# Gate and up of two feed-forward layers, from the fifth feature tile on, as pairs of output tiles by seven half-size products

## The chip, the cores and the metric

One core of a Trainium2 chip runs the whole program. The time is the device time of one execution, in microseconds. Profiles come from one further execution.

## What is computed

A decoder layer on 512 tokens of width 1024: a half-weighted SwiGLU feed-forward layer (FFN1), two parallel attention mixers, cross-attention to a memory of 256 rows, a second SwiGLU layer (FFN2), and a last norm. Only the two feed-forward layers change. D_FF is 2816.

```python
def swiglu(h, w_gate, w_up, w_down):
    return (jax.nn.silu(h @ w_gate) * (h @ w_up)) @ w_down
...
x = x + 0.5 * swiglu(rms_norm(x, norm_ffn1[l]), w1_gate[l], w1_up[l], w1_down[l])
...
x = x + 0.5 * swiglu(rms_norm(x, norm_ffn2[l]), w2_gate[l], w2_up[l], w2_down[l])
return rms_norm(x, norm_final)
```

## The kernel before

The activations lie transposed, features on the 128 partitions and the 512 tokens along the columns. A weight tile `w1_gate[f]` is 128 x 1024: for each of 8 k blocks of the input, the 128 output features of tile f. There are 22 feature tiles, FT.

Every product keeps float32 accuracy in three passes. An operand is split into a high half (a cast to float32r on ScalarE, L77) and a low half (a subtraction on VectorE, L78), and high x high, high x low, low x high are added up in one PSUM bank (`dense_steps`, L94 to L104). `wload` (L84) loads a weight tile on SP's queue into one of three raw buffers `wr` and splits it in pieces of 512 columns into `wh`, `wl` (two buffers each); it is given a priority 40 instructions ahead.

In `ffn` (L204) a feature tile is 24 matmuls of 512 columns for gate and 24 for up, with the weights stationary and `xh`, `xl` moving. `xh`, `xl` are x times the norm's gain, split (L201, L202); the norm's row factor `rb` is applied afterwards: t1 = gate x rb (L217), Silu (L219), times rb (L220), times up (L223), split into `ah`, `al`. The down part then makes 8 output tiles m, each from 66 matmuls: 22 f x 3 passes. In FFN2 the last output tile is made in two halves of 256 tokens (L234 to L241) and the final norm follows each half (`finish`, L946).

The homes of the tiles matter below. Group B (`big`, L70) has 30 buffers of 2 KB a partition: x, and of `ah`, `al` those with f < 11. The other `ah`, `al` are in the FFN's own pool (L205, L210). `xh`, `xl` have 16 tiles of their own (L137, L138).

A scheduler sets each engine's order at build time: by readiness, and among what is ready by place in the program, less the priority. An engine then takes its instructions in that order. In the trace, for example, the first matmuls of the mixing stage stand ahead of the sums of the norm before it.

`tables` (L276) is FFN1's hook. After tile 5 it makes bias tables with four small matmuls (L297), copies them from PSUM (L298), writes them to DRAM (L299, L300) and spreads them there to 128 rows a head, `fa_r` and `fb_r` (L301, L302), all on POOL's queue. After FFN1 x goes to DRAM (`x_d`, L307), and the mixing stage projects `xh`, `xl` with w_in.

Of the kernel before, what the change touches and what calls it, by code (L numbers as in the profile page):

```python
# [9 lines left out]
F32 = mybir.dt.float32  # L10
F32R = mybir.dt.float32r
AF = mybir.ActivationFunctionType
ALU = mybir.AluOpType
# [19 lines left out]
VC = 408  # L33
DOWN = (8, 8, 6)
OFF = (0, 128, 384, 768)
NB = 30
AHEAD = 40
LB = 3
PB = 3
# [9 lines left out]

SLOT_A = "STSffTSfPSTSfPTffPfP"  # L50
SLOT_B = "fSSfTTSfffPP"
GRP = ((0,), (1,), (2, 3))


@with_exitstack
def hybrid_layer(ctx: ExitStack, tc: tile.TileContext, a: dict):
# [13 lines left out]
    def big(dt, name):  # L70
        return g.tile([P, S], dt, tag="B", name=name, bufs=NB)

# [33 lines left out]
    def dense(*args):  # L106
        for _ in dense_steps(*args):
            pass
# [29 lines left out]
    xl = [g.tile([P, S], F32R, name=f"xl{k}") for k in range(KT)]  # L138

    class Norm:  # L140
        def __init__(self, width, tag, nsq=1, tsq=None, tacc=None):
# [62 lines left out]
    def ffn(pool, tag, rb, nrm, gi, first=None, hook=None, done=None):  # L204
        def act(n):  # L205
            return pool.tile([P, S], F32R, tag="act", name=n, bufs=2 * FT - (NB - KT))

        ah, al = [], []
        for f in range(FT):
            mk = act if 2 * f >= NB - KT else (lambda n: big(F32R, n))  # L210
            ah.append(mk("ah"))
            al.append(mk("al"))
            pg, pu = bank("d"), bank("d")
            fg, fu = first if first and f == 0 else (None, None)
            dense(pg, [(a[f"w{tag}_gate"][f], KT)], xh, xl, fg)
            t1 = pool.tile([P, S], F32, tag="t1", name="t1", bufs=2)
            V.tensor_mul(t1, pg, rb())  # L217
            s1 = pool.tile([P, S], F32, tag="s1", name="s1", bufs=2)
            A.activation(s1, t1, AF.Silu)  # L219
            V.tensor_mul(s1, s1, rb())  # L220
            dense(pu, [(a[f"w{tag}_up"][f], KT)], xh, xl, fu)
            ac = pool.tile([P, S], F32, tag="ac", name="ac", bufs=2)
            V.tensor_mul(ac, pu, s1)  # L223
            split(ah[f], al[f], ac)
            if hook:
                hook(f)
        for m in range(KT):
            pd = bank("d")
            src = a[f"w{tag}_down"][m]
            ch, o = [], 0  # L230
            for n in DOWN:
                ch.append((src[:, o * P:(o + n) * P], n))
                o += n
            if done and m == KT - 1:  # L234
                for c0 in (0, S // 2):
                    c = slice(c0, c0 + S // 2)
                    dense(pd[:, :S // 2], ch, [t[:, c] for t in ah], [t[:, c] for t in al])
# [19 lines left out]
    with tc.tile_pool(name="f1", bufs=1, reuse_waits="tile") as pool:  # L257
        first = [wpair(), wpair()]

        def part(i, c0, c1):  # L260
            h, l = first[i]
            split(h[:, c0:c1], l[:, c0:c1], raw0[i][:, c0:c1])

        part(0, 0, 256)
        for k in range(KT):
            scale_split(xh[k], xl[k], x[k], gain(0, k))
            if k < 3:
                part(*((1, 0, 256), (0, 256, 1024), (1, 256, 1024))[k])
        n1 = Norm(S, "x", 3)
        for k in range(KT):  # L270
            n1.feed(pool, x[k])
        n1.finish()

        tb = {}

        def tables(f):  # L276
            if f == 0:
                tb["rel"] = pool.tile([33, 16], F32, name="rel")
                tb["oh32"] = pool.tile([P, FA + FB], F32, name="oh32")
                nc.gpsimd.dma_start(tb["rel"], a["rel"])  # L280
                nc.gpsimd.dma_start(tb["oh32"], a["oh"])
            if f != 5:
                return
            rel, oh32 = tb["rel"], tb["oh32"]
            rr = pool.tile([P, 16], F32R, name="rr")
            oh = pool.tile([P, FA + FB], F32R, name="oh")
# [644 lines left out]
        n4.finish()  # L931


    n5 = Norm(S, "x", 3)
    with tc.tile_pool(name="f2", bufs=1, reuse_waits="tile") as pool:
        gx = []
        halves = [[], []]

        def turn(half, i, ks):
            if len(halves[half]) <= i:  # L940
                halves[half].append(bank(("ssot", "ddds")[half][i]))
            for k in ks:
                c = (k - 4 * half) * P
                T.transpose(halves[half][i][:, c:c + P], gx[k][:, i * P:(i + 1) * P], ident)  # L944

        def finish(c0):  # L946
            c = slice(c0, c0 + S // 2)
            tiles = range(c0 // P, c0 // P + 2)
            m = KT - 1
            sq = pool.tile([P, S // 2], F32, tag="sqx", name="sq", bufs=3)  # L950
            A.activation(sq, x[m][:, c], AF.Square)
            V.tensor_scalar(gx[m][:, c], x[m][:, c], gain(4, m), None, op0=ALU.mult)
            for i in tiles:
                turn(1, i, range(4, m))
            st = n5.sums2(sq, c0)
            for i in tiles:
                turn(1, i, (m,))
            r = n5.rstd(st, 2)
            for i in tiles:
                o = pool.tile([P, D], F32, tag="out", name="out", bufs=2)  # L960
                rr = r[:, i % 2:i % 2 + 1]
                A.activation(o[:, :512], halves[0][i], AF.Copy, scale=rr)
                V.tensor_scalar(o[:, 512:], halves[1][i], rr, None, op0=ALU.mult)  # L963
                if c0:
                    nc.scalar.dma_start(a["out"][i * P:(i + 1) * P, :512], o[:, :512])
                    nc.sync.dma_start(a["out"][i * P:(i + 1) * P, 512:], o[:, 512:])
                else:
                    (nc.sync if i % 2 else nc.scalar).dma_start(a["out"][i * P:(i + 1) * P, :], o)

        def done(m, c0=0):  # L970
            if c0 == 0:
                gx.append(pool.tile([P, S], F32, tag=("t1", "t1", "s1", "s1", "ac", "ac", "t1", "t1")[m],
                                    name="gx", bufs=2))
# [9 lines left out]
        ffn(pool, "2", lambda: n4.rb, n5, None, done=done)  # L983


OUT = (S, D)
# [94 lines left out]
```

## Time and profile before

| | us |
|---|---|
| median of 3 runs | 1292.76 (1291.57 to 1292.77) |
| the profiled execution, its own time | 1293.45 |
| its span | 1291.4 |
| TensorE busy | 1272.5 |
| VectorE busy | 717.4 |
| ScalarE busy | 569.0 |
| 139 MB moved by DMA, mean | 108 GB/s |

FFN1 lies at 5 to 377 us of the span, the mixing stage from there to 751, cross-attention to about 917, FFN2 after it. Matmul rows overlap, so TensorE's pace is read from the distance between two starts, not from a row's length. A row of the timeline may merge several instructions (x2).

### The profile page before, as it was taken

Reading aid. Unit: us, or ns where it says so; the run is one execution under the profiler, and the core shown is the slowest. Engines: PE = TensorE matmul, PEld = TensorE weight load, DVE = VectorE, ACT = ScalarE, POOL = GpSimd, SP = SyncE. Lnnn points to the kernel's source line nnn. Section 1 sums busy time; section 2 is a strip of 40 time slices with the busy share of each in tenths; the row PEclk is TensorE's granted clock in tenths of the full one; section 3 lists DMA queues with packets and bytes.
Section 4 is the critical chain, followed back from the end, with each engine's and each line's share of the span. In section 5 each row is a group of like instructions: output and inputs, shape, how many; then the busy total and the mean of one; then the engine's idle time right before and its main releaser. Section 6 shows DMA issues by size and latency. Waiting matters only on the chain. (4 is left out here: it accounts for less than half of the span.)

```text
span 1291.4 us, 16177 instructions
## 1 busy us (share of the span) xinstructions
PE 1272.5 (99%) x6092; PEld 1057.6 (82%) x6092; DVE 717.4 (56%) x1510; ACT 569.0 (44%) x1178; POOL 29.9 (2%) x56
## 2 busy tenths in 40 slices
PE   7999999999999999999999999999999999999997
PEld 5888888888887888888888898887888888888887
DVE  5554444433348787887878666465544444443334
ACT  6333333322234677776784454444433333322223
POOL 0000000000020000000001000000000000000000
PEclk9999999999999999999999999999999999999999
DMA  5346333233343531222225345212233333332233
GB/s 205 98 131 236 97 98 97 93 118 111 106 142 97 177 97 65 88 71 70 62 92 164 111 137 173 82 50 82 82 98 98 98 98 98 98 94 90 90 97 116
DMA packets 41199, 139.11 MB, mean 108 GB/s; under 512 B 6248, under 2 KB 6512, under 8 KB 41120
## 3 DMA queue, kind: packets, MB, share of 16 engines
q1 hardware_dynamic: 34704, 120.04, 29.6%
q0 software_dynamic: 5840, 16.95, 3.8%
q8 instruction: 48, 0.79, 0.2%
q10 hardware_dynamic: 576, 1.07, 0.2%
q14 instruction: 31, 0.25, 0.1%
HBM read 133.80 MB, written 10.07 MB: 111 GB/s over the span
## 5 line engine op out<-in xcount | busy, mean ns | idle before, releaser
L77 ACT ACTIVATE wh<-wr 128x512 fp32r<-128x512 f32 (+1 forms) x456 | 259.8, 614 | 598.0 <-issue 389.3
L102 PE MATMUL ps_d<-xh,wh 128*128 128x512 f32 x1000 | 393.1, 394 | 8.0 <-ACT xh L201 8.0
L102 PE MATMUL ps_d<-xh,wl 128*128 128x512 f32 x1000 | 393.0, 393 | 1.7 <-DVE wl L78 1.7
L102 PE MATMUL ps_d<-xl,wh 128*128 128x512 f32 x1000 | 391.9, 392 | 0.0
L78 DVE TENSOR_TENSOR wl<-wr,wh 128x512 fp32r<-128x512 f32 (+1 forms) x456 | 291.5, 674 | 150.9 <-ACT wh L77 148.7
L102 PEld LDWEIGHTS ps_d<-xh,wh 128*128 128x128 f32 x1000 | 188.6, 189 | 46.3 <-ACT xh L201 9.4
L102 PEld LDWEIGHTS ps_d<-xh,wl 128*128 128x128 f32 x1000 | 188.6, 189 | 39.3 <-DVE wl L78 2.1
L102 PEld LDWEIGHTS ps_d<-xl,wh 128*128 128x128 f32 x1000 | 188.4, 188 | 38.1 <-DVE xl L202 1.0
L102 PE MATMUL ps_d<-ah,wl 128*128 128x512 f32 (+1 forms) x374 | 142.3, 380 | 0.0
L102 PE MATMUL ps_d<-al,wh 128*128 128x512 f32 (+1 forms) x374 | 142.2, 380 | 0.0
L102 PE MATMUL ps_d<-ah,wh 128*128 128x512 f32 (+1 forms) x374 | 142.0, 380 | 0.0
L223 DVE TENSOR_TENSOR ac<-ps_d,s 128x512 f32<-128x512 f32 x44 | 30.4, 691 | 123.1 <-PE ps_d L102 123.1
L217 DVE TENSOR_TENSOR t<-ps_d,rb 128x512 f32<-128x512 f32 x44 | 30.4, 691 | 123.0 <-PE ps_d L102 120.7
L102 PEld LDWEIGHTS ps_d<-al,wh 128*128 128x128 f32 x374 | 70.3, 188 | 14.4
L102 PEld LDWEIGHTS ps_d<-ah,wh 128*128 128x128 f32 x374 | 70.3, 188 | 14.3
L102 PEld LDWEIGHTS ps_d<-ah,wl 128*128 128x128 f32 x374 | 70.3, 188 | 13.9
L481 ACT ACTIVATE pth<-ps_t 128x512 fp32r<-128x512 f32 (+1 forms) x64 | 32.6, 524 | 18.3 <-PE ps_t L586 15.4
L482 DVE TENSOR_TENSOR ptl<-ps_t,pth 128x512 fp32r<-128x512 f32 (+1 forms) x64 | 37.8, 602 | 3.5 <-ACT pth L481 2.8
L542 DVE CUSTOM_DVE_ANT_0 L<-ps_s,strA 128x512 f32<-128x512 f32 (+1 forms) x64 | 31.0, 485 | 13.5 <-PE ps_s L499 13.3
L544 ACT ACTIVATE L<-L,ms 128x512 f32<-128x512 f32 (+1 forms) x64 | 35.5, 556 | 6.1 <-DVE ms L542 5.9
L498 PE MATMUL ps_s<-kkh,qs 128*128 128x256 f32 (+7 forms) x104 | 31.6, 320 | 0.3 <-DVE ms L542 0.3
L220 DVE TENSOR_TENSOR s<-s,rb 128x512 f32<-128x512 f32 x44 | 30.1, 684 | 1.3 <-ACT s L219 1.3
(268 smaller groups left out, 1553.1 us busy)
## 6 DMA issues: line engine op xcount, KB each, us to landing
wr<-in_w_gate_dram SPq DMA_DIRECT2D x43, 512.0 KB, 3.5
wr<-in_w_up_dram SPq DMA_DIRECT2D x43, 512.0 KB, 3.5
wr<-in_w_down_dram SPq DMA_DIRECT2D x34, 512.0 KB, 3.5
wr<-in_w_in_dram SPq DMA_DIRECT2D x29, 512.0 KB, 3.5
wr<-in_w_down_dram SPq DMA_DIRECT2D x17, 384.0 KB, 3.0
fa_r<-fa_d POOLq DMA_DIRECT2D x1, 4160.0 KB, 34.2
wr<-in_cw_dram SPq DMA_DIRECT2D x8, 512.0 KB, 3.6
wr<-in_w_out_dram SPq DMA_DIRECT2D x8, 512.0 KB, 3.6
```

The lines of the kernel that those rows point to most:

```text
L77: A.activation(h, src, AF.Copy)
L78: V.tensor_sub(l, src, f32(h))
L102: yield T.matmul(out, w[:, c], m, start=i == 0, stop=i == total - 1)
L217: V.tensor_mul(t1, pg, rb())
L220: V.tensor_mul(s1, s1, rb())
L223: V.tensor_mul(ac, pu, s1)
L481: A.activation(h[:, :n], pt[:, :n], AF.Copy)
L482: V.tensor_sub(l[:, :n], pt[:, :n], f32(h[:, :n]))
L498: first = T.matmul(out, q[:, tk], kk[0][:, ks], start=True, stop=False)
L542: V.tensor_tensor_reduce(sl, sc, hd["strip"][:, (3 - i) * P:512], -1.0, BIG, ALU.add, ALU.min, ms[:, i:i + 1])
L544: A.activation(sl, sl, AF.Exp, bias=ms[:, i:i + 1], scale=-1.0, accum_out=ss[:, i:i + 1])
```

## The change

In both FFNs the feature tiles 0 to 3 are made as before. From tile 4 on two neighbouring feature tiles f, f+1 are taken together. The product of a 2 x 2 block matrix (two output tiles by two halves of the input features, 4 k blocks each) with a 2 x 2 block matrix (two halves of the input features by two halves of the tokens, 256 each) is made from seven products of blocks instead of eight. A product is 4 k x 3 passes = 12 matmuls of 256 columns. There are 18 such steps q in an FFN, gate and up in turn.

The blocks of the activations, their sums and the halves of both are made once, after tiles 0 and 1 (`prepare`); they contain gain and rb, so nothing is multiplied by rb later. Blocks b11, b21, b22 lie in group B, the sums t3, t4, n2, n1 in the pool's new tag E. The sums of weight blocks are made per step: two by a load (`s31`, from SP) onto which a second load is added by a DMA with an add, from POOL's queue, and two by additions on VectorE (`s2`, `s4`). The weights of a step are split in 3584 columns, not 2048. Partial products are used twice, so ScalarE copies them from bank to bank and the matmuls go on from there; two matmuls ahead of the loop prepare the two banks.

Group B has 46 buffers instead of 30 and also holds `xh`, `xl`, which are given up after tile 3 and made again at the end of FFN1, and `ah`, `al` with f < 15. The tables of FFN1 are made after tile 1 instead of tile 5, in three parts. The down part makes its tiles 0 and 1 side by side, chunk by chunk.

```diff
-NB = 30
+NB = 46
+NE = 23
+NSTD = 4
+NEARLY = 4
...
-    xh = [g.tile([P, S], F32R, name=f"xh{k}") for k in range(KT)]
+    xh = [big(F32R, f"xh{k}") for k in range(KT)]
...
+        def prepare(i):
+            ys = []
+            for k0 in (2 * i, 2 * i + 4):
+                y = pool.tile([P, 1024], F32, tag="S", name="y", bufs=3)
+                for j in range(2):
+                    V.scalar_tensor_tensor(y[:, j * S:(j + 1) * S], x[k0 + j], gain(gin, k0 + j), nrm_in.rb,
+                                           op0=ALU.mult, op1=ALU.mult)
+                ys.append(halves(y))
...
+            V.tensor_sub(v["n1"], ta, tb_)
+            V.tensor_sub(v["t3"], bb, tb_)
+            V.scalar_tensor_tensor(v["n2"], v["n1"], -1.0, bb, op0=ALU.mult, op1=ALU.subtract)
+            V.scalar_tensor_tensor(v["t4"], v["n2"], -1.0, ba, op0=ALU.mult, op1=ALU.subtract)
+            for n, src in (("b11", ta), ("b21", ba), ("b22", bb)):
+                h, l = big(F32R, n), big(F32R, n)
+                A.activation(halves(h), src, AF.Copy)
+                V.tensor_sub(halves(l), src, halves(f32(h)))
+            for n in ("t3", "t4", "n2", "n1"):
+                h, l = ext(n, F32R), ext(n, F32R)
+                split(h, l, sums[n])
...
+        def load(q):
...
+            nc.sync.dma_start(d["r1"], w[f])
+            d["s"] = pool.tile([P, 1024], F32, tag="S", name="s31", bufs=3)
...
+            nc.sync.dma_start(s31, bass.AP(o.tensor, o.offset, [[1024, P], [0, 2], [1, 512]]))
+            o = w[f]
+            nc.gpsimd.dma_start(s31, bass.AP(o.tensor, o.offset, [[1024, P], [P * 1024 + 512, 2], [1, 512]]),
+                                accum_op=ALU.add)
...
+        def product(out, w, c0, n, start=False):
+            i = 0
+            for k in range(4):
+                c = slice(c0 + k * P, c0 + (k + 1) * P)
+                bh, bl = (t[:, k % 2 * 256:k % 2 * 256 + 256] for t in blk[n][k // 2])
+                for ww, m in ((w[0], bh), (w[0], bl), (w[1], bh)):
+                    T.matmul(out, ww[:, c], m, start=start and i == 0, stop=i == 11, skip_group_check=True)
+                    i += 1
...
+        load(0)
+        load(1)
+        load2(0)
+        for _ in range(2):
+            t = bank("s")
+            T.matmul(t, xh[0][:, :P], xl[0], start=True, stop=True, skip_group_check=True)
+        s2(0)
+        h1(0)
+        h2(0)
+        early = list(range(NEARLY))
+        for q in range(NQ + 1):
...
+            if d:
+                x_, g_ = bank("d")[:, :256], bank("s")
+                product(x_, d["h1"], 0, "b11", True)
+                A.activation(g_[:, :256], x_, AF.Copy)
+                h3(q)
+                if q + 2 < NQ:
+                    load(q + 2)
+                if q + 1 < NQ:
+                    s2(q + 1)
+                p7 = bank("o")[:, :256]
+                product(p7, d["h2"], 0, "t3", True)
...
+                if q + 1 < NQ:
+                    h1(q + 1)
+            if e:
+                join_b(q - 1)
+                product(e["x"], e["h4"], 512, "t4")
+                join_a(q - 1)
+            if d:
+                s4(q)
+                product(x_, d["h2"], 512, "n2")
+                A.activation(g_[:, 256:], x_, AF.Copy)
+                if q + 1 < NQ:
+                    h2(q + 1)
+                product(g_[:, :256], d["h1"], 512, "b21")
+            if e:
+                product(e["g"][:, 256:], e["h4"], 0, "b22")
+                out_g(q - 1)
+            if d:
+                h4(q)
+                if q + 1 < NQ:
+                    load2(q + 1)
+                if early:
+                    act_split(early.pop(0))
+                product(g_[:, 256:], d["h3"], 0, "n1")
...
+        if not done:
+            for m in range(KT):
+                xh[m], xl[m] = big(F32R, f"xh{m}"), big(F32R, f"xl{m}")
+                scale_split(xh[m], xl[m], x[m], gain(gi, m))
...
-            if f != 5:
+            if f != 1:
```

`h1` to `h4` split the weights of a step (h1: the whole tile f, 1024 columns; h2: 2 x 512; h3: 512; h4: 1024), `join_a` and `join_b` add the copied product p7 in halves of 256 columns, `out_g` makes Silu or the product with it for tile f, and `load2` loads 256 KB of tile f+1 for h4. h2, h3, h4 have one buffer each, tag S has three.

## Rows read from the trace of the kernel before

**Rows 1.** The page: busy time of the engines (us, share of the span, instructions)

```profile
PE 1272.5 (99%) x6092; PEld 1057.6 (82%) x6092; DVE 717.4 (56%) x1510; ACT 569.0 (44%) x1178; POOL 29.9 (2%) x56
```

**Rows 2.** Timeline, TensorE in FFN1's gate and up: start, length, engine, line, operation

```profile
99.70 0.39 PE L102 MATMUL ps_d<-xh,wh 128*128 128x512 f32 x1
...
121.46 0.39 PE L102 MATMUL ps_d<-xh,wh 128*128 128x512 f32 x1
```

**Rows 3.** Stretches of FFN1: busy time of each engine, clock, DMA share, GB/s

```profile
88.00:125.00 37.00, 37.00 (x165) 30.65 (x164) 16.44 (x27) 10.65 (x20) 2.18 (x2) 1.00 0.75 258
125.00:200.00 75.00, 75.00 (x333) 62.10 (x332) 34.91 (x56) 23.34 (x42) 0.00 (x0) 1.00 0.30 95
```

**Rows 4.** Timeline, 256 columns in FFN2's last down tile; weight loads of the key projection

```profile
1264.96 0.28 PE L102 MATMUL ps_d<-ah,wh 128*128 128x256 f32 x1
...
1268.82 0.28 PE L102 MATMUL ps_d<-ah,wh 128*128 128x256 f32 x1
...
1272.65 0.28 PE L102 MATMUL ps_d<-ah,wl 128*128 128x256 f32 x1
...
L102 PEld LDWEIGHTS ps_d<-gh,wh x64: 187/188/192, 751.4 to 776.0; 128*128 128x128 f32 x64
```

**Rows 5.** Timeline, 512 columns in FFN2's down tile 6

```profile
1249.74 0.40 PE L102 MATMUL ps_d<-ah,wh 128*128 128x512 f32 x1
...
1257.45 0.40 PE L102 MATMUL ps_d<-ah,wh 128*128 128x512 f32 x1
...
1259.53 0.39 PE L102 MATMUL ps_d<-ah,wh 128*128 128x512 f32 x1
...
1264.51 0.39 PE L102 MATMUL ps_d<-al,wh 128*128 128x512 f32 x1
```

**Rows 6.** Groups by line and shape: one of three groups of 1000 with `xh`, `xl`

```profile
L102 PE MATMUL ps_d<-xh,wh 128*128 128x512 f32 x1000 | 393.1, 394 | 8.0 <-ACT xh L201 8.0
```

**Rows 7.** Groups by shape on VectorE and ScalarE (busy us, mean ns); two timeline rows

```profile
L78 DVE TENSOR_TENSOR wl<-wr,wh 128x512 fp32r<-128x512 f32 x431 | 281.4, 686 | 148.3 <-ACT wh L77 146.1 <-PE ps_o L494 1.6
L77 ACT ACTIVATE wh<-wr 128x512 fp32r<-128x512 f32 x431 | 250.7, 624 | 597.6 <-issue 389.3 <-PE ps_d L102 182.4 <-PE ps_d L855 9.8
L579 ACT ACTIVATE pth<-ps_t 128x256 fp32r<-128x256 f32 x8 | 3.0, 371 | 0.6 <-PE ps_t L577 0.6
...
14.34 3.40 DVE L202 SCALAR_TENSOR_TENSOR xl<-x,gains,xh 128x512 fp32r<-128x512 f32 x5
37.79 1.28 DVE L78 TENSOR_TENSOR wl<-wr,wh 128x512 fp32r<-128x512 f32 x2
```

**Rows 8.** Timeline, VectorE in FFN2: first use of rb, and output of tile 3

```profile
923.95 0.69 DVE L217 TENSOR_TENSOR t<-ps_d,rb 128x512 f32<-128x512 f32 x1 [0.47 <-ACT rb L193]
...
960.75 0.69 DVE L223 TENSOR_TENSOR ac<-ps_d,s 128x512 f32<-128x512 f32 x1 [2.95 <-PE ps_d L102]
```

**Rows 9.** Timeline, VectorE in FFN1: first use of rb, outputs of tiles 1 and 3

```profile
29.84 0.69 DVE L217 TENSOR_TENSOR t<-ps_d,rb 128x512 f32<-128x512 f32 x1 [1.88 <-ACT rb L193]
...
37.18 0.69 DVE L223 TENSOR_TENSOR ac<-ps_d,s 128x512 f32<-128x512 f32 x1 [1.15 <-PE ps_d L102]
...
58.94 0.69 DVE L223 TENSOR_TENSOR ac<-ps_d,s 128x512 f32<-128x512 f32 x1 [2.94 <-PE ps_d L102]
```

**Rows 10.** The tables: timeline of TensorE and POOL, then DMA issues (KB, us to landing)

```profile
80.50 0.63 PE L297 MATMUL ps_t<-oh,rr 128*8 128x512 f32 x2
...
88.84 1.09 POOL L301 DMA_DIRECT2D fa_r<-fa_d  x1 [3.04 <-DMA fa_d<-fa]
90.07 1.09 POOL L302 DMA_DIRECT2D fb_r<-fb_d  x1
...
fa_r<-fa_d POOLq DMA_DIRECT2D x1, 4160.0 KB, 34.2
fb_r<-fb_d POOLq DMA_DIRECT2D x1, 1536.0 KB, 33.8
wr<-in_w_gate_dram SPq DMA_DIRECT2D x43, 512.0 KB, 3.5
```

More of the change, by code (lines that the diff above doesn't have):

```diff
@@ L135, in hybrid_layer @@
     V.memset(ones, 1.0)
-    xh = [g.tile([P, S], F32R, name=f"xh{k}") for k in range(KT)]
-    xl = [g.tile([P, S], F32R, name=f"xl{k}") for k in range(KT)]
+    xh = [big(F32R, f"xh{k}") for k in range(KT)]
+    xl = [big(F32R, f"xl{k}") for k in range(KT)]
     class Norm:
@@ L202, in scale_split, with ffn, ext, act_split @@
         V.scalar_tensor_tensor(l, src, gcol, f32(h), op0=ALU.mult, op1=ALU.subtract)
[L204 to L212, printed above, removed]
+    def ffn(pool, tag, nrm_in, gin, nrm, gi, first=None, hook=None, done=None):
+        def ext(name, dt=F32):
+            return pool.tile([P, S], dt, tag="E", name=name, bufs=NE)
+        wsrc = {"g": a[f"w{tag}_gate"], "u": a[f"w{tag}_up"]}
+        act, ah, al = [None] * FT, [None] * FT, [None] * FT
+        def act_split(f):
+            ah[f], al[f] = (big(F32R, n) if f < 15 else ext(n, F32R) for n in ("ah", "al"))
+            split(ah[f], al[f], act[f])
+        blk = {n: [None, None] for n in ("b11", "b21", "b22", "n1", "t3", "n2", "t4")}
+        def halves(t):
+            return t.rearrange("p (j c) -> p j c", j=2)
+        def prepare(i):
[6 more added lines that the diff above has]
+                ys.append(halves(y))
+            yt, yb = ys
+            ta, tb_, ba, bb = yt[:, :, :256], yt[:, :, 256:], yb[:, :, :256], yb[:, :, 256:]
+            sums = {n: big(F32, n + "s") for n in ("n1", "t3", "n2", "t4")}
+            v = {n: halves(t) for n, t in sums.items()}
+            V.tensor_sub(v["n1"], ta, tb_)
[6 more added lines that the diff above has]
+                V.tensor_sub(halves(l), src, halves(f32(h)))
+                blk[n][i] = h, l
+            for n in ("t3", "t4", "n2", "n1"):
+                h, l = ext(n, F32R), ext(n, F32R)
+                split(h, l, sums[n])
+                blk[n][i] = h, l
+        for f in range(NSTD):
@@ L213, in ffn @@
             pg, pu = bank("d"), bank("d")
             fg, fu = first if first and f == 0 else (None, None)
[L215 to L218, printed above, removed]
+            dense(pg, [(wsrc["g"][f], KT)], xh, xl, fg)
+            t1 = ext("t1")
+            V.tensor_mul(t1, pg, nrm_in.rb)
+            s1 = ext("s1")
@@ L219, in ffn @@
             A.activation(s1, t1, AF.Silu)
[L220 to L224, printed above, removed]
+            V.tensor_mul(s1, s1, nrm_in.rb)
+            dense(pu, [(wsrc["u"][f], KT)], xh, xl, fu)
+            act[f] = big(F32, "act")
+            V.tensor_mul(act[f], pu, s1)
             if hook:
                 hook(f)
-        for m in range(KT):
-            pd = bank("d")
-            src = a[f"w{tag}_down"][m]
+            if f in (0, 1):
+                prepare(f)
@@ new lines, in load2, with hl, s2, s4 @@
+        def load2(q):
+            w, f = pairs[q]
+            q_[q]["r2"] = pool.tile([P, 1024], F32, tag="R2", name="r2", bufs=1)
+            nc.sync.dma_start(q_[q]["r2"][:, 512:], wsrc[w][f + 1][:, 512:])
+        def hl(tag_, n):
+            return tuple(pool.tile([P, n], F32R, tag=tag_ + z, name=tag_ + z, bufs=1) for z in "hl")
+        def s2(q):
+            d = q_[q]
+            d["s2"] = ext("s2")
+            V.tensor_add(d["s2"], d["s"][:, 512:], d["r1"][:, :512])
+        def s4(q):
+            d = q_[q]
+            V.tensor_add(d["r2"][:, :512], d["s2"], d["r1"][:, 512:])
@@ L230, in ffn, with chunks, finish_m @@
+        def chunks(m):
             ch, o = [], 0
             for n in DOWN:
-                ch.append((src[:, o * P:(o + n) * P], n))
+                ch.append((a[f"w{tag}_down"][m][:, o * P:(o + n) * P], n))
                 o += n
+            return ch
+        def finish_m(m, pd):
+            V.scalar_tensor_tensor(x[m], pd, 0.5, x[m], op0=ALU.mult, op1=ALU.add)
+            if done:
+                done(m)
+            else:
+                nrm.feed(pool, x[m])
+        two = [bank("d"), bank("d")]
@@ new lines, in ffn @@
+        o = 0
+        for c, n in enumerate(DOWN):
+            ws = [wload(*(lambda z: (z[0], z[1] * P))(chunks(m)[c])) for m in range(2)]
+            for f in range(o, o + n):
+                if ah[f] is None:
+                    act_split(f)
+            for m in range(2):
+                h, l = ws[m]
+                for kk in range(n):
+                    cc = slice(kk * P, (kk + 1) * P)
+                    f = o + kk
+                    for z, (w, v) in enumerate(((h, ah[f]), (h, al[f]), (l, ah[f]))):
+                        T.matmul(two[m], w[:, cc], v, start=f == 0 and z == 0, stop=f == FT - 1 and z == 2)
+            o += n
@@ L234, in ffn @@
+        for m in range(2):
+            finish_m(m, two[m])
+        for m in range(2, KT):
+            pd = bank("d")
             if done and m == KT - 1:
@@ L949, in finish @@
             m = KT - 1
-            sq = pool.tile([P, S // 2], F32, tag="sqx", name="sq", bufs=3)
+            sq = pool.tile([P, S], F32, tag="E", name="sq", bufs=NE)[:, :S // 2]
             A.activation(sq, x[m][:, c], AF.Square)
@@ L959, in finish @@
             for i in tiles:
-                o = pool.tile([P, D], F32, tag="out", name="out", bufs=2)
+                o = pool.tile([P, D], F32, tag="S", name="out", bufs=3)
                 rr = r[:, i % 2:i % 2 + 1]
@@ L971, in done @@
             if c0 == 0:
-                gx.append(pool.tile([P, S], F32, tag=("t1", "t1", "s1", "s1", "ac", "ac", "t1", "t1")[m],
-                                    name="gx", bufs=2))
+                gx.append(big(F32, "gx"))
             if m == KT - 1:
@@ L981, in done @@
                     turn(0, i, range(4))
-        ffn(pool, "2", lambda: n4.rb, n5, None, done=done)
+        ffn(pool, "2", n4, 3, n5, None, done=done)
 OUT = (S, D)
```

105 lines of the change are left out of this document (79 added, 26 removed).

## The prediction

> **What bounds the kernel now.** I read the page first: TensorE is busy for 1272.5 us, 99% of the span [rows 1], and its granted clock is 1.00 in the stretches that I read [rows 3]. A busy matmul row is no measure of pace, because the rows overlap (394 ns long, while a new one starts every 227 ns), so next I took start-to-start pitches from the timeline. In gate and up, 96 consecutive pitches take 121.46 - 99.70 = 21.76 us, 226.7 ns each, without a hole [rows 2]. That stretch is bound by TensorE alone: what shortens the matmul stream shortens the kernel, until something else comes late. VectorE works 34.9 of 75 us there, ScalarE 23.3, the DMA engines 30% [rows 3].
>
> The profiled execution took 1293.45 us, 0.7 above the median 1292.76; the sum is made against it and 0.7 is taken off at the end.
>
> **The matmul stream.** Per FFN, 18 of the 22 feature tiles become 9 pairs, each for gate and for up: 18 steps. A step had 2 x 24 = 48 matmuls of 512 columns, 48 x 226.7 ns = 10.88 us. It gets 7 products x 4 k x 3 passes = 84 of 256 columns. The kernel has such matmuls already. In FFN2's last down tile the first 33 start from 1264.96 to 1268.82, 117.0 ns apart; their moving halves `ah`, `al` (f < 11) lie in group B. The next 32 pitches, to 1272.65, are 119.7 ns; those halves lie in the FFN pool [rows 4]. After the change three moving blocks (b11, b21, b22) lie in B and four (t3, t4, n2, n1) in the pool's tag E, so I take 36 x 116.8 + 48 x 119.9 ns = 9.96 us a step. It saves 0.92 us, **36 steps: -33.1 us**, where the bare count of columns (1/8 of 36 x 10.88) would promise 49: the pitch at half width is more than half. A weight load row before a matmul of that width is 188 ns long [rows 4], yet these matmuls follow each other in 117, so loads overlap and don't set the pace.
>
> The Trainium skill (TensorE: Matmul & The Clock Gate, Back-to-back issue gap) gives N/2.4 + 2.5 ns, which is 109 and 216 ns here. By it the steps would save 36 x (48 x 215.8 - 84 x 109.2 ns) = 42.7 us. The trace differs at both widths, so the rows' pitches stand.
>
> **The moving operand's home.** `xh` and `xl` had tiles of their own and now come from group B. At 512 columns B is the slower home: in down tile 6 of FFN2 the 33 matmuls from B take 1257.45 - 1249.74 = 7.71 us, 233.6 ns each, those from the pool 4.98/22 = 226.4 [rows 5], as with `xh` in its own tiles [rows 2]. There are 3 x 1000 matmuls with `xh` or `xl` [rows 6]; the FFNs hold 2112, of which 384 stay (four tiles), and 888 are in w_in and w_xq. So 1272 x 6.7 ns = **+8.5 us**; nothing if it isn't the group that makes it. `ah`, `al` for f 11 to 14 move to B as well: 4 x 3 x 8 x 6.7 ns = 0.64 a FFN, **+1.3**. Two warm-up matmuls a FFN: **+0.9**.
>
> **Inside a step.** VectorE: a 512-column subtraction is 0.69 us, 0.60 behind another (two take 1.28) [rows 7]. A step has seven for the low halves, two sums, two joins of half the width (0.35, half of 0.69) and one output on average: 6.7 to 7.6 of 9.96 us. ScalarE: 7 x 0.62 + 3 x 0.37 + 0.62 = 6.1. Both fit. A copy of a partial product has at least two products (2.8 us) until the next accumulation. The tightest is h4: its buffer is free after product b22, it is read three products (4.3 us) later, and it needs a Silu (0.62), a cast of 1024 (two of 0.62 at most) and a subtraction (1.2), 3.1 us. It is covered, except in the last step, where only n1 (1.4 us) lies between: **+1.2 a FFN, +2.4** (0 to 4).
>
> The loads become 1.75 MB a step (512 KB whole, 512 KB base, 512 KB added to it from POOL's queue, 256 KB), 184 GB/s against 95 at 30% [rows 3]: 58% of the engines if an adding byte costs as a plain one, 75% at twice. No row shows an adding DMA; plain is the nearest (3.5 us for 512 KB [rows 10]). I take twice, which adds nothing to the sum, as plain wouldn't; four times is rival 3. SP's queue is used in order, but the loads are issued a step ahead.
>
> **The end of FFN1.** `xh`, `xl` take the buffers of `ah`, `al`, so their scaling comes after the last down tile. The next stage's matmuls need them one k block after another; half of the 16 buffers are free before that, the others as tile 7 reads them. I take 0, at worst 3.
>
> **The start of FFN2.** rb is there at 923.95, tile 3 ends at 960.75 [rows 8]: 36.8 us. VectorE owes 12 operations x 0.6 for the four tiles, five weight tiles x 1.2, the `prepare` work (2 x (6 x 0.68 + 9 x 0.60) = 19.0, the 0.68 being 3.40 us for five [rows 7]) and the first sums and halves (1.8): 34.0. It fits: **+0.5** (0 to 3).
>
> **The start of FFN1.** There rb comes when tile 1 is nearly done: 29.84, and tile 3 ends at 58.94 [rows 9], 29.1 us. VectorE owes 7.2 + four weight tiles 4.8 + 19.0 + table copies 2.0 + 1.8 = 34.8. `prepare(0)` stands ahead of tile 2's weight split, so TensorE waits there: **+5.5** (3 to 8). The steps then begin at 58.94 + 1.3 (slower home) + 5.5 = 65.7.
>
> **The table copies.** The tables move from tile 5 to tile 1. Today tile 5 ends at 80.3, the first table matmul is at 80.50, fa_r and fb_r go out at 88.84 and 90.07, and fa_r lands 34.2 us later, at 123.0 [rows 10]. fb_r, issued 1.2 us after it and a third its size, lands 33.8 us later, with it: POOL's DMAs end behind one another. Tile 1 ends at 37.2 [rows 9]; with the copies behind `prepare(0)` (some 4 us) the tables go out near 49 and land near 84. The adding DMAs use this same queue. That of step 1 needs a buffer of tag S, three in all, which `prepare(1)` holds until past 50, then its base load (3.5 us): it is issued behind fa_r and lands near 85. Product t3 of step 1 would start at 65.7 + 6 x 1.42 = 74.2 and needs h2, some 1.5 us after that landing: **+12** (0 to 20). TensorE's queue holds everything else behind that product.
>
> Sum: -33.1 + 8.5 + 1.3 + 0.9 + 2.4 + 0.5 + 5.5 + 12 = -2.0: 1291.4 profiled, **1290.7 us** (1285 to 1296 alone).
>
> **Rivals.** (1) The adding DMAs don't wait for the tables: the scheduler has issued them earlier, or the queue lets them pass. For: the DMA engines are at 75%, not full, while the tables go out [rows 3]. Against: fb_r's landing. Without the 12: **1278.7**.
> (2) Slower: the adding DMA of step 0 is caught as well. It decides if fa_r is issued before step 0's base load has landed (about 46 against 49). Then step 0's t3 waits from 67.1 to 86, 19 instead of 12: **1297.7**, against 1292.8 before.
> (3) Adding DMAs cost four times a plain byte: 108% of the engines, a step lasts 10.76 us, 36 x 0.8 = 29 us more: **1320**. For: a third operand has to be read; against: the loads run at 3.5 us for 512 KB with room. The Trainium skill (Collectives: The Full Stack, The bandwidth ceiling) says that an add in the DMA path reads two sources and halves the rate; no run here shows it yet. By that the engines would be at 75% and the sum would stay.
>
> **How the numbers follow.** Forecast 0.44, rival 1 0.28, rival 2 0.18, rival 3 0.06, waits between products that I don't see 0.04. The range goes from rival 1 with part of the +8.5 gone (1274) to rival 2 with its own error (1302). A measurement here tells 0.2%, 2.6 us, from no change. Rival 1 is faster; of the forecast 0.21 is faster, 0.14 same, 0.09 slower; rival 2 gives 0.04 same, the rest slower: faster 0.49, same 0.18, slower 0.33.
>
> **What the profile after would show.** Right: 84 matmuls of 256 columns at 117 and 120 ns, steps of 9.96 us, `xh` at 233.5 ns in the mixing stage, one hole of TensorE around 74 to 86 us released by an adding DMA, a smaller one at tile 2. Wrong: steps clearly longer than 10 us (then VectorE's or the DMA engines' share tells which), no hole in FFN1 (rival 1), a hole from 67 (rival 2), or `xh` still at 226.7 (8.5 us better).

## The result, and the profile after

The changed kernel takes 1301.09 us (median of 4 runs, 1300.39 to 1301.76) against 1292.76 (1291.57 to 1294.10) before: ratio 1.0064, 95% interval 1.0047 to 1.0081. It is slower, by 8 us; the prediction was 1290.7. The profiled execution has a span of 1299.5 us. Its page, busy time by engine and the clock granted in 40 slices (rows of before: [rows 1]):

```profile
span 1299.5 us, 19405 instructions
PE 1260.8 (97%) x7392; PEld 1101.1 (85%) x7392; DVE 847.7 (65%) x1678; ACT 674.0 (52%) x1352; POOL 75.6 (6%) x96
PEclk9979999999999999999999999999989999999999
```

TensorE is busy for 11.7 us less than before, and the span is 8.1 us longer: the time is in holes, and in two slices (65 to 97 us and 942 to 975) the clock is down. By stages, from the timelines (us from the start of the span):

| stretch, up to | before | after | change | forecast |
|---|---|---|---|---|
| end of tile 3 / first Strassen product, FFN1 | 58.94 | 64.63 | +5.7 | +7.2 |
| first matmul of the down tiles alone | 255.42 | 264.84 | +3.7 | -3.4 |
| first use of FFN2's rb | 923.95 | 934.25 | +0.9 | +6.6 |
| end of tile 3 / first Strassen product, FFN2 | 960.75 | 980.22 | +9.2 | +2.2 |
| first matmul of the down tiles alone, FFN2 | 1156.39 | 1165.04 | -10.8 | -15.3 |
| end of the span | 1291.4 | 1299.5 | -0.6 | +0.7 |
| sum | | | +8.1 | -2.0 |

**FFN1's holes.** TensorE's timeline at the two holes, what ScalarE and VectorE did at their ends, and the issues that they waited for:

```profile
67.35 0.28 PE L333 MATMUL ps_o<-t,h2l 128*128 128x256 f32 x1
71.88 0.80 PE L333 MATMUL ps_d<-n,h2h 128*128 128x256 f32 x2 [4.25 <-ACT ps_s L381]
...
83.13 0.28 PE L333 MATMUL ps_d<-b,wl 128*128 128x256 f32 x1
90.07 0.79 PE L333 MATMUL ps_o<-t,h2h 128*128 128x256 f32 x2 [6.66 <-ACT p L390]
...
69.55 1.06 ACT L81 ACTIVATE wh<-wr 128x1024 fp32r<-128x1024 f32 x1 [6.09 <-DMA wr<-in_w_up_dram]
71.46 0.36 ACT L381 ACTIVATE ps_s<-ps_d 128x256 f32<-128x256 f32 x1
89.06 0.69 DVE L300 TENSOR_TENSOR s<-s,wr 128x512 f32<-128x512 f32 x1 [8.66 <-DMA s<-in_w_up_dram]
...
52.60 1.13 POOL L517 DMA_DIRECT2D fa_r<-fa_d  x1 [2.14 <-DMA fa_d<-fab]
58.06 1.26 POOL L286 DMA_DIRECT2D s<-in_w_up_dram  x1 [3.23 <-DVE wl L82]
56.28 0.34 SPq L280 DMA_DIRECT2D wr<-in_w_up_dram  x1
```

The same three issues in the DMA view (KB each, us to landing):

```profile
fa_r<-fa_d POOLq DMA_DIRECT2D x1, 4160.0 KB, 33.3
s<-in_w_up_dram POOLq DMA_DIRECT2D x1, 512.0 KB, 31.0
wr<-in_w_up_dram SPq DMA_DIRECT2D x1, 512.0 KB, 13.2
```

fa_r goes out at 52.6 and lands at 85.9; the adding DMA of step 1, issued at 58.06 behind it, lands at 89.0, and product t3 of step 1 starts 1 us later. That is the predicted hole, a few us later than predicted. The other one is new: SP's load for the same step takes 13.2 us instead of 3.5 ([rows 10]), and ScalarE stands for 6.1 us before its cast. Two places behind that cast is a seed copy: so the text calls the two copies of a step that fill one half of a bank from another bank (L381 behind b11, L401 behind n2). n2 adds to the bank from which L381 reads, so it waits for it. Behind both holes TensorE is slow (stretches: busy time and count by engine, granted clock, DMA share, GB/s):

```profile
72.00:78.00 6.00, 6.00 (x28) 6.00 (x29) 2.20 (x3) 1.26 (x3) 0.00 (x0) 0.50 1.05 350
90.10:95.00 4.90, 4.90 (x23) 4.90 (x24) 3.45 (x7) 1.97 (x4) 0.00 (x0) 0.50 0.76 200
967.00:972.00 5.00, 5.00 (x13) 3.89 (x13) 4.46 (x8) 0.63 (x1) 0.49 (x1) 0.50 1.06 176
```

After it had stood still, the granted clock is 0.50, the lower of its two levels (1.2 instead of 2.4 GHz). The 28 matmuls from 71.88 to 78.05 take 6.17 us instead of 3.3, the 24 from 90.07 to 95.28 take 5.21 instead of 2.85: 5.2 us on top of holes of 4.4 and 6.8.

**FFN2's start.** TensorE's timeline, then ScalarE's in order, then VectorE's:

```profile
960.95 0.39 PE L106 MATMUL ps_d<-xl,wh 128*128 128x512 f32 x1
966.11 0.80 PE L106 MATMUL ps_d<-xh,wl 128*128 128x512 f32 x1 [4.77 <-DVE wl L82]
...
955.14 0.63 ACT L81 ACTIVATE wh<-wr 128x512 fp32r<-128x512 f32 x1 [0.65 <-PE ps_d L106]
...
957.76 0.62 ACT L244 ACTIVATE b<-y 128x512 fp32r<-128x512 f32 x1
963.58 0.63 ACT L81 ACTIVATE h2h<-s 128x512 fp32r<-128x512 f32 x1 [5.20 <-DMA s<-in_w_gate_dram]
964.12 0.61 ACT L81 ACTIVATE n<-n2s 128x512 fp32r<-128x512 f32 x1
...
964.76 0.69 DVE L82 TENSOR_TENSOR n<-n2s,n 128x512 fp32r<-128x512 f32 x1 [5.34 <-ACT n L81]
965.37 0.69 DVE L82 TENSOR_TENSOR wl<-wr,wh 128x512 fp32r<-128x512 f32 x1
```

TensorE waited for the low half of tile 3's gate weights (965.37 on VectorE). The cast that it is made from had been done since 955.77. But on VectorE it stood behind the low half of n2, which waited for ScalarE's cast of n2 (964.12). That cast stood behind the one of step 0's h2, before which ScalarE waited 5.2 us for an adding DMA (landed at 963.56). So one late load passed through two queues; the expectations below put the cast of tile 3's weights behind the h2 cast, which it isn't here. Hole 4.9 us, slow clock 2.9 (14 matmuls in 6.14 us; the expectation below counts 15).

**A steady step.** Product b11 of the same kind starts at 1008.00 and, 14 steps later, at 1150.90: 10.21 us a step (10.15 in FFN1), where 9.96 was forecast. One border of each step, TensorE and ScalarE:

```profile
1003.43 0.28 PE L333 MATMUL ps_d<-n,h2l 128*128 128x256 f32 x1
1003.55 0.40 PE L333 MATMUL ps_s<-b,h4h 128*128 128x256 f32 x2
...
1003.63 0.63 ACT L81 ACTIVATE h2h<-s 128x512 fp32r<-128x512 f32 x1 [2.38 <-PE ps_d L333]
1004.17 0.37 ACT L401 ACTIVATE ps_s<-ps_d 128x256 f32<-128x256 f32 x1
...
1004.26 0.40 PE L333 MATMUL ps_s<-b,h4h 128*128 128x256 f32 x2
1004.59 0.50 PE L333 MATMUL ps_s<-b,wh 128*128 128x256 f32 x2
```

n2 ends at 1003.43; ScalarE first does a cast for the next step and then the seed copy (L401), which ends at 1004.54; b21 (`b,wh`) starts at 1004.59, after eight matmuls of b22. From 1004.38, the second of the row at 1004.26, to 1004.59 is 0.21 us in place of 0.12, and the restart costs another 0.1. By the code b21 adds to columns 0 to 255 of its bank, which L381 had filled long before, and L401 fills columns 256 to 511: b21 doesn't need what the copy brings, it waits because the two share a bank.

### The profile page after: what moved, and what is told of

Its sections match the earlier page's. It is cut to its first block, busy times and chain, and to the rows that moved or that the text cites. A ratio compares the mean times of both kernels' runs of the same rounds, so it can differ in the third digit from the quotient of the medians.

```text
span 1299.5 us, 19405 instructions
## 1 busy us (share of the span) xinstructions
PE 1260.8 (97%) x7392; PEld 1101.1 (85%) x7392; DVE 847.7 (65%) x1678; ACT 674.0 (52%) x1352; POOL 75.6 (6%) x96
## 5 line engine op out<-in xcount | busy, mean ns | idle before, releaser
L81 ACT ACTIVATE wh<-wr 128x512 fp32r<-128x512 f32 (+2 forms) x348 | 215.6, 656 | 347.8 <-PE ps_d L106 156.7
L82 DVE TENSOR_TENSOR wl<-wr,wh 128x512 fp32r<-128x512 f32 (+2 forms) x348 | 242.8, 728 | 173.2 <-ACT wh L81 173.0
L106 PE MATMUL ps_d<-xh,wh 128*128 128x512 f32 x424 | 171.2, 405 | 13.6 <-ACT xh L205 13.6
L106 PE MATMUL ps_d<-xh,wl 128*128 128x512 f32 x424 | 172.1, 406 | 5.4 <-DVE wl L82 5.4
L106 PE MATMUL ps_d<-xl,wh 128*128 128x512 f32 x424 | 170.3, 402 | 0.0
L106 PEld LDWEIGHTS ps_d<-xh,wh 128*128 128x128 f32 x424 | 80.9, 191 | 29.6 <-ACT xh L205 13.6
L106 PEld LDWEIGHTS ps_d<-xh,wl 128*128 128x128 f32 x424 | 81.1, 191 | 23.0 <-DVE wl L82 6.3
L106 PEld LDWEIGHTS ps_d<-xl,wh 128*128 128x128 f32 x424 | 80.9, 191 | 17.8 <-DVE xl L206 1.3
L333 PE MATMUL ps_d<-n,h2h 128*128 128x256 f32 x288 | 55.3, 290 | 4.2 <-ACT ps_s L381 4.2
L333 PE MATMUL ps_s<-b,wh 128*128 128x256 f32 x288 | 57.0, 296 | 0.1
```

The source lines that it names most:

```text
L106: yield T.matmul(out, w[:, c], m, start=i == 0, stop=i == total - 1)
L333: T.matmul(out, ww[:, c], m, start=start and i == 0, stop=i == 11, skip_group_check=True)
```

## Experiments

### The table work behind the last step

`ffn` calls its hook once more behind the loop of steps, and `tables` does both of its parts then:

```diff
                 product(g_[:, 256:], d["h3"], 0, "n1")
+        if hook:
+            hook(-1)
...
-            if f == 0:
+            if f == -1:
...
-            if f != 1:
+            if f != -1:
```

> The changed kernel (1301.1 us, ratio 1.0064 to the kernel before) with the whole table work of FFN1 (loads, matmuls, copies, fa_r and fb_r) moved behind the last Strassen step. Theory: the two holes of TensorE in FFN1 (67.35 to 71.88 and 83.13 to 90.07 us, 11.2 us without the normal pitch) and the slow clock behind them (28 matmuls in 6.17 us after the first, 24 in 5.21 after the second, 5.2 us over their normal pace) come from fa_r and fb_r, which take the DMA engines and stand ahead of the adding DMA on POOL's queue. Then both go, about -16.4 us: 1284.7. Rival: the first steps' loads are late by themselves (buffers, SP's order), and the tables only coincide: the holes stay, 1298 or more.

Measured: 1293.35 us, ratio to before 1.0003 (0.9993 to 1.0013). In FFN1 the theory holds: the steps end at 248.55 instead of 264.72 us, 16.2 earlier, 2.8 of them ahead of the first step. Of the two large holes one is left, of 1.8 us:

```profile
66.60 0.50 PE L333 MATMUL ps_d<-n,h2h 128*128 128x256 f32 x2 [1.76 <-ACT ps_s L381]
```

But 2.6 us were given back in the down tiles, where the table work now lies, and 7.0 in the mixing stage (from the last down tile to the first product with `mh`: 336.7 instead of 329.7 us). There this kernel has a stretch in which VectorE is full and TensorE waits for its weight splits:

```profile
409.00:419.00 10.00, 4.56 (x21) 3.51 (x20) 9.78 (x20) 5.77 (x13) 0.00 (x0) 0.92 0.00 1
```

VectorE's work on the tiles F has piled up there: in the 36.5 us ahead VectorE is busy for 19.8, at the same place in the changed kernel for 32.8. Why it starts later wasn't followed further. The rival is out, but for the 1.8 us left.

### The tables from ScalarE's queue

```diff
-            nc.gpsimd.dma_start(fa_r, fa_d.unsqueeze(1).to_broadcast([8, P, FA]))
-            nc.gpsimd.dma_start(fb_r, fb_d.unsqueeze(1).to_broadcast([8, P, FB]))
+            nc.scalar.dma_start(fa_r, fa_d.unsqueeze(1).to_broadcast([8, P, FA]))
+            nc.scalar.dma_start(fb_r, fb_d.unsqueeze(1).to_broadcast([8, P, FB]))
```

> The changed kernel with fa_r and fb_r issued from ScalarE's queue at the same time instead of POOL's. Tells the queue from the bandwidth. If the order on POOL's queue makes the second hole: the adding DMA of step 1 (issued 58, landed 89.0) lands within some 12 us, the hole at 83 goes with its slow clock (-9.2 us), the hole at 67, behind a plain load of SP that takes 13 us, stays: 1292. If only the shared DMA engines make it: that DMA still lands past 80, both holes stay: 1301.

Measured: ratio 1.0141 (1.0123 to 1.0159), 10 us slower than the changed kernel. On the question asked: the adding DMA of step 1, issued at 75.16, lands 10.8 us later, not 31. The tables were still under way: their queue moved 0.88 MB while that DMA was in flight, and went on past 100 us (DMA view). So it overtook them, and the long wait was the order in POOL's queue. (It was issued 24 us behind the tables here, 5.5 before.) The time was lost elsewhere (ScalarE's timeline):

```profile
52.58 11.63 ACTq L518 DMA_DIRECT2D fb_r<-fb_d  x1
64.59 0.63 ACT L244 ACTIVATE b<-y 128x512 fp32r<-128x512 f32 x1 [14.83 <-issue]
```

The issue of fb_r held ScalarE for 11.6 us (on POOL it took 1.1), and TensorE had a hole of 11.4 us at 58.35. Both expectations missed this.

### Scratch of prepare elsewhere

```diff
-                y = pool.tile([P, 1024], F32, tag="S", name="y", bufs=3)
+                y = pool.tile([P, 1024], F32, tag="h4" + "hl"[z], name="y", bufs=1)
```

> The changed kernel with the scratch tiles y of prepare in the buffers of h4 instead of tag S, so that the base and adding loads of the first three steps can go out at once. Theory: the hole of FFN2 at 960.95 to 966.11 us (4.9 us, and 2.9 of slow clock behind it: 15 matmuls of 512 columns in 6.14 us) is ScalarE's queue: the cast of step 0's h2 waits there for the adding DMA (landed 963.56) with the cast of tile 3's weights behind it. With the load early it goes: -7.8. In FFN1 the adding DMAs of steps 0 to 2 go out ahead of fa_r, so the hole at 83 goes too (-9.2), the one at 67 may stay: 1284 in all. Rival: FFN2's hole is VectorE's debt of 34.0 us of work in 36.8: that hole stays, 1292.

Measured: 1284.31 us, 0.9929 (0.9912 to 0.9945). The sum is as expected, its parts are not: FFN1's steps end 15.7 us earlier (both large holes are gone), but FFN2 from rb to the end of the steps gains 2.0 only (229.6 instead of 231.6). The load is early now, and so is the cast that waits for it:

```profile
927.70 0.63 ACT L81 ACTIVATE h2h<-s 128x512 fp32r<-128x512 f32 x1 [6.83 <-DMA s<-in_w_gate_dram]
...
928.76 1.14 ACT L81 ACTIVATE wh<-wr 128x512 fp32r<-128x512 f32 x2
...
932.12 0.79 PE L106 MATMUL ps_d<-xh,wl 128*128 128x512 f32 x1 [1.96 <-DVE wl L82]
```

The hole has moved from 961 to 928 and 930 us. It is the same queue; whether VectorE's debt lies beneath it was still open.

### Step 0's casts held back

On top of the last one. The cast of `split` gets a scale, 1 worked out from tile 2's output; h3 and s2 of step 0 get it too:

```diff
+                d["one"] = pool.tile([P, 1], F32, name="one", bufs=1)
+                V.tensor_scalar(d["one"], act[NSTD - 2][:, :1], 0.0, 1.0, op0=ALU.mult, op1=ALU.add)
...
-            split(h[:, :512], l[:, :512], d["s"][:, :512])
+            split(h[:, :512], l[:, :512], d["s"][:, :512], d.get("one"))
```

> The run with y elsewhere (1284.3) and, on top of it, the casts of step 0 (h2, h3 and the sum s2) held back until tile 2 is finished, by a factor 1 worked out from its output. Theory: FFN2's hole, which had only moved from 961 to 930 us, is ScalarE's queue waiting for the adding DMA; from rb to the end of the steps FFN2 took 229.6 us, of which the two known costs leave 222.0 (218.6 by the sum, 3.4 by the seed copy): up to -7.6, 1276.7. Rival: VectorE's debt (34.0 of 36.8 us): the hole moves to prepare's halves and the time stays at 1284.

Measured: 1278.38 us, 0.9884 (0.9869 to 0.9899), 5.9 less than without. FFN2 has no hole above 0.5 us between rb and the steps' end, which are 222.8 us apart (222.0 expected). So the hole came from the h2 cast that waited in ScalarE's queue, and VectorE's 34 us do fit into FFN2's 36.8. Two things are not in the theory: 1.0 us of FFN2's gain lies in the steps (10.15 instead of 10.21 us each), and FFN1's steps end 1.5 us later (250.5 instead of 249.0). Neither was followed further.

### h2 in two tiles

```diff
-            h, l = d["h2"] = hl("h2", 1024)
+            d["h2"], d["h2b"] = hl("h2", 512), hl("i2", 512)
```

> The changed kernel with h2 as two tiles of 512 columns, one read by product t3 and one by n2, so that the first half's cast for the next step need not wait for n2. Theory: in every step ScalarE does this cast (0.54 us) ahead of the seed copy on which product b21 waits; two products then take 3.03 to 3.08 instead of 2.82 us. With the cast earlier the step goes from 10.16 to about 9.97 us: -6.8 us over 36 steps: 1294.3. Rival: the lost 0.2 us belongs to the switch of banks or weights between b22 and b21, and not to the copy: step and time stay, 1301.

Measured: 1301.81 us, 1.0066 (1.0051 to 1.0081): no change. But the edit didn't bring about what it was for. Another cast, of the second half, took the place ahead of the seed copy:

```profile
1004.43 0.64 ACT L81 ACTIVATE i2h<-s 128x512 fp32r<-128x512 f32 x1 [1.98 <-PE ps_d L333]
1004.97 0.37 ACT L401 ACTIVATE ps_s<-ps_d 128x256 f32<-128x256 f32 x1
```

It decides nothing between the two theories.

### b22 ahead of b21

```diff
+            if e:
+                product(e["g"][:, 256:], e["h4"], 0, "b22")
+                out_g(q - 1)
             if d:
                 product(g_[:, :256], d["h1"], 512, "b21")
-            if e:
-                product(e["g"][:, 256:], e["h4"], 0, "b22")
-                out_g(q - 1)
```

> The changed kernel with product b22 of the step before placed whole ahead of b21, so that TensorE has 12 matmuls (1.42 us) instead of 8 between n2 and the product that needs the seed copy. (Two tiles for h2 had not moved the cast out of ScalarE's way, so that run left the question open.) Theory: b21 waits for the seed copy, which ends 1.15 us after n2's last matmul starts, behind a cast. Then b22 and b21 together go from 3.03 to 3.08 us to 2.82, the step from 10.16 to 9.97: 36 x 0.19 = -6.8 us, 1294.3. Rival: the loss belongs to the switch of products: it stays at the new border, 1301.

Measured: 1295.18 us, 1.0014 (1.0005 to 1.0023): -5.9 us. ScalarE's order is as before, but its copy is done in time (TensorE's b22 goes on to 1003.26, b21 follows at the normal pitch):

```profile
1002.04 0.63 ACT L81 ACTIVATE h2h<-s 128x512 fp32r<-128x512 f32 x1 [2.38 <-PE ps_d L333]
1002.58 0.37 ACT L401 ACTIVATE ps_s<-ps_d 128x256 f32<-128x256 f32 x1
...
1003.26 0.28 PE L333 MATMUL ps_s<-b,h4l 128*128 128x256 f32 x1
1003.38 0.40 PE L333 MATMUL ps_s<-b,wh 128*128 128x256 f32 x2
```

14 steps take 1146.22 - 1006.22 = 140.0 us, 10.00 each, 9.95 in FFN1: the 9.96 of the prediction. The switch of products costs nothing.

### The home of the moving tiles

```diff
+    g.tile([P, 8], F32, name="pad0")
     x = [big(F32, f"x{k}") for k in range(KT)]
+    g.tile([P, 8], F32, name="pad1")
```

The first pad moves B by 32 bytes; the second is meant to keep the place of what follows as it was, counted in steps of 64 bytes.

> The changed kernel with group B moved by 32 bytes in SBUF (all else stays where it is). Theory: the pitch follows the place of the moving operand's tile, and the old tiles of xh and xl lay as the moved B does. Then the 512-column matmuls from B go from 233.5 to 226.7 ns (1272 with xh or xl, 720 with ah or al in B: -13.3 us), the 256-column ones of b11, b21 and b22 from 116.8 to 119.9 (1296: +4.1): 1291.9. Rival: the pitch belongs to something else in B (who wrote the tile, the sharing of buffers): 1301.

Measured: 1293.09 us, 0.9999 (0.9990 to 1.0008): -8.0. 97 consecutive matmuls of FFN2's down tiles, first and last, here:

```profile
1165.96 0.39 PE L446 MATMUL ps_d<-ah,wh 128*128 128x512 f32 x1
...
1187.72 0.39 PE L106 MATMUL ps_d<-ah,wh 128*128 128x512 f32 x1
```

96 pitches in 21.76 us, 226.7 ns; in the changed kernel the 35 from 1165.73 to 1173.90 are 233.4 ns each. The blocks in B went the other way, to 120.0. So the place makes the difference, in either direction, and not what else belongs to B. Whether it is the place by itself or its distance to the weight tile wasn't tried; the run with all repairs shows that the moving tile's place is not all. The time gained is short of the sum in part because the three holes grew, by 3.0 us together (5.67, 6.96 and 6.09 us idle instead of 4.25, 6.66 and 4.77): what ends them are DMAs, which don't land earlier when TensorE is faster.

The same pads in the kernel before:

> The kernel before with its group B moved by 32 bytes: how much of the home repair the kernel before would have had too. 2 FFNs x 8 down tiles x 33 matmuls of 512 columns from B at 226.7 instead of 233.5 ns: -3.6 us, the last down tile's 66 half-width ones +0.2, other tiles of B in the mixing stages unknown, nothing to -4: 1285 to 1289. If the place of the tile doesn't matter in this kernel: 1292.8.

Measured: 1286.76 us, 0.9954 (0.9940 to 0.9969), -6.3, within what was left open. The kernel before could have had this, too.

### A plain load for the adding one

```diff
-                                accum_op=ALU.add)
```

> The changed kernel with the adding loads as plain ones (the sums of weight blocks are left out, so the output is not the reference's). Prices the adding by itself. If an adding byte costs twice a plain one, the DMA engines' share in the steady steps falls from 0.65 by 0.1 to 0.2, the load lands in about 5.0 us (like SP's of the same size there) instead of 5.8, and the time stays, 1301, for the steps don't wait for it. If the steps were bound by adding, they would get shorter than 10.16 us.

Measured in one run: 1296.75 us. The DMA view of the stretch 1000 to 1150 us, POOL's queue (packets, MB, share of 16 engines), here and in the changed kernel:

```profile
q0 software_dynamic: 1872, 6.82, 15.8%
```

```profile
q0 software_dynamic: 3536, 6.82, 28.9%
```

Seven of the loads in it, plain and adding:

```profile
s<-in_w_up_dram POOLq DMA_DIRECT2D x7, 512.0 KB, 4.0
```

```profile
s<-in_w_up_dram POOLq DMA_DIRECT2D x7, 512.0 KB, 5.9
```

Adding takes 5.9 us instead of 4.0, and the same 6.82 MB take 28.9% of the engines instead of 15.8: an added byte costs 1.8 times a plain one. The Trainium skill (Collectives: The Full Stack, The bandwidth ceiling) gives two; the trace agrees nearly. The step stays at 10.21 us: it doesn't wait for adding. The 4 us, which the expectation didn't have, came from the starts, where a load is waited for: FFN1's steps end 1.7 us earlier, and FFN2's begin another 2.8 earlier.

### All four repairs, and the start

y elsewhere, step 0's casts held back, b22 first, B moved:

> All four repairs together: y elsewhere, step 0's casts held back, b22 ahead of b21, B moved by 32 bytes. If they add: 1301.1 - 16.8 - 7.6 - 6.8 - 9.2 = 1260.7. If TensorE's pace now runs into another engine (VectorE 69% busy in the steps, the DMA engines 65%), less: 1270.

Measured: 1260.95 us, 0.9753 (0.9736 to 0.9769). No other engine has become the bound. That it comes so near to 1260.7 is in part luck: that sum was made of forecasts, and the four gains as measured (16.8 + 5.9 + 5.9 + 8.0 = 36.6) are 3.5 us short of the 40.1 that they give together. Most of the 3.5 lies in FFN1's steps, 9.89 us each, less than the 9.95 with b22 first alone, although the moved B should make them longer. TensorE there, the first matmuls of b22, of b21 and of n1:

```profile
138.00 0.39 PE L341 MATMUL ps_s<-b,h4h 128*128 128x256 f32 x2
...
139.37 0.40 PE L341 MATMUL ps_s<-b,wh 128*128 128x256 f32 x2
...
140.80 0.40 PE L341 MATMUL ps_s<-n,h3h 128*128 128x256 f32 x2
```

b22's 12 matmuls are 114 ns apart and b21's 119, though both move blocks of B; in FFN2 b22 takes 120 too. So the weight tile has a part in the pitch. Its place may be the reason (y and the new tile `one` rearranged that pool), which wasn't tried apart.

Against the kernel before with the same pads it is 0.9753/0.9954 = 0.980.

On top of it, the order at the very start:

```diff
-    xh = [big(F32R, f"xh{k}") for k in range(KT)]
+    xh = [g.tile([P, S], F32R, name=f"xh{k}") if k < 4 else big(F32R, f"xh{k}") for k in range(KT)]
```

with 42 buffers in B instead of 46.

> The run with all four repairs (1260.9), and the first four xh tiles in buffers of their own (B has 42 instead of 46), which puts their scaling ahead of the squares on ScalarE as in the kernel before. Theory A: the late first matmul (11.71 us here, 13.57 in the changed kernel, 4.95 before) costs what it seems: the Strassen steps start near 59 instead of 62.3: 1258. Theory B, the term of the prediction: the squares then come later, rb with them (28.0 instead of 21.7 us), and VectorE owes 34.8 us of work in the time from rb to the end of tile 3: TensorE waits there instead, the steps start at 62 to 65.7: 1261 to 1264.

Measured: 1266.81 us, 0.9801 (0.9784 to 0.9817), 5.9 slower. The first matmul is 6.0 us earlier (5.75), but behind it TensorE waits 6.0 us for VectorE's `xl`, so this run gains nothing at the start and can't decide on theory A. rb is 2.7 later (24.32 instead of 21.67, by the norm's transposes), and the steps begin 3.1 later, at 65.36. TensorE at the start and at the first weights of tile 3, and VectorE:

```profile
12.93 0.80 PE L106 MATMUL ps_d<-xl,wh 128*128 128x512 f32 x1 [5.97 <-DVE xl L208]
...
51.46 0.40 PE L106 MATMUL ps_d<-xh,wl 128*128 128x512 f32 x1
54.79 0.50 PE L106 MATMUL ps_d<-xh,wl 128*128 128x512 f32 x1 [2.93 <-DVE wl L82]
...
53.45 0.68 DVE L82 TENSOR_TENSOR n<-n1s,n 128x512 fp32r<-128x512 f32 x1
54.05 1.28 DVE L82 TENSOR_TENSOR wl<-wr,wh 128x512 fp32r<-128x512 f32 x2
```

The 2.9 us are theory B's: tile 3's weight split stands behind the halves of `prepare(1)` on VectorE, and TensorE waits for it. It is the kind of wait that the prediction had for the changed kernel, there at tile 2 behind `prepare(0)`. Some 2.7 us of the loss come later, 1.4 of them as a hole in the mixing stage (at 647.4); B's four tiles less may be its cause, which wasn't tried apart.

## Why the prediction was wrong, point by point

- **The matmul stream: right.** 84 matmuls at 117 and 120 ns make 9.96 us; without the wait at b21 the step is 9.95 to 10.00. The back-to-back figure of the Trainium skill (TensorE: Matmul & The Clock Gate, Back-to-back issue gap) gives an estimate of 84 x 109 ns = 9.2; the runs differ, and they decide. The 9.96 itself holds for the homes of this kernel: with other homes the steps took 9.89 to 10.02.
- **Inside a step: wrong, +6.8 us.** "A copy of a partial product has at least two products until the next accumulation" counts the next product that adds to the half which the copy fills (n1). But b21, which follows at once, adds to the other half of the same bank, and it waited for the copy. And the step took ScalarE's sum (6.1 of 9.96 us), not its order: a cast that becomes free at the same instant goes first. b22 ahead of b21 gave 5.9 back.
- **The table copies: right in kind, 4.4 short.** POOL's order was the cause, and fa_r landed at 85.9 (forecast 84). The holes are 11.2 us (forecast 12), but one of them came by SP's loads at 13 us, and the 5.2 us at the lower clock weren't in the sum. SP's load was slow while the DMA engines were full (1.05 in the stretch 72 to 78, where rows 3 had 0.75); that the tables filled them is shown by the run without them, in which that hole shrinks to 1.8 us.
- **The start of FFN2: wrong, +0.5 forecast, 7.8 found.** VectorE's sum was right; the wait was on ScalarE, of whose queue the prediction counted no order at all. Its own rule, to name what is queued behind a waiting instruction, would have found it: the h2 cast waits for an adding DMA, the cast of n2 is behind it, and on VectorE tile 3's weight split is behind the low half of n2.
- **The start of FFN1: right sum, other cause.** +5.7 against 7.2, but no wait at prepare. The change put the squares of the norm ahead of xh on ScalarE, so the first matmul is at 13.57 instead of 4.95 (3.0 us of that take the place of a second wait for `xh` that the kernel before had), and rb is used at 26.52 instead of 29.84 [rows 9]; with the early rb VectorE's debt is paid in time. The last experiment shows a wait from that debt, of 2.9 us, when rb is late. That the sum came out near is luck.
- **The moving operand's home: right, but not seen in the table.** The undoing is worth 8.0 us, 9.2 by the sum. From FFN1's last down tile to FFN2's rb it gave 5.1 back, where before to after shows only +1.4 (546.8 and 548.2 us): something else there became some 4 us shorter with the change. About 1 us of it is idle time of TensorE (2.2 instead of 3.3 us from the first down tile on); what the rest is stays open.
- **Chances.** The rival on the slow side had its place in step 0's adding DMA, which in fact landed at 54.9. That the result lies near that rival's 1297.7 is chance. Two waits on ScalarE, 14 us together, had been in "waits between products that I don't see", at 0.04.

## What to carry to other kernels

An engine that fits by its sum can still cost: write down the order of its queue at each border, and ask of every instruction that waits for a DMA who stands behind it. Price a long hole of TensorE with the slow matmuls that follow it: behind the three of this kernel they cost half as much again. Not every hole has them: behind 2.9 us in the last run the granted clock was 1.00, behind 2.0 us at 932 in the run with y elsewhere it was 0.50. When one thing is made faster, look at what it then waits for: the holes grew when only the matmuls got faster. Where the speed of an operation depends on where its tile lies, a change that moves tiles is priced by that too, and 32 bytes of padding can matter: by themselves they gave 8 us, where the repaired kernel is 40 us ahead of the changed one.

## What the runs showed of the hardware

- The pitch of back-to-back matmuls depends on where the operands lie: the group of the moving tiles moved by 32 bytes turned 233.4 into 226.7 ns at 512 columns and 116.7 into 120.0 at 256. The moving tile is not all: with blocks of the same group, 256 columns took 114 and 119 ns with different weight tiles.
- A load of 512 KB that adds takes 5.9 us and 1.8 times the engines' time of a plain one (4.0 us).
- Behind holes of 4.4, 6.8 and 4.9 us the granted clock was 0.50, which cost another 2.9, 2.4 and 2.9 us.
- A small DMA behind a large one on POOL's queue: 512 KB landed 31.0 us after the issue, 3 us behind 4.1 MB issued 5.5 us ahead of it; with the large one on another queue it took 10.8 us.
- Issuing a second large DMA from ScalarE's queue held that engine for 11.6 us.
